# Two nested branches in an expert's further slots: the false arm named as the one to fall through to

## The chip, the cores and the metric

The kernel runs on one core of a Trainium2 chip. The metric is the device time of one execution in microseconds. Before the change three runs took 1592.51, 1592.9 and 1587.8 us, a median of 1592.51.

## The reference

The program is a decoder trunk of two layers over 256 tokens of width 1024, in float32. Each layer has a token mixer (two kinds of attention with a gated merge) and then a feed-forward part; layer 0 has a dense SwiGLU, layer 1 eight SwiGLU experts of inner width 3584, of which each token uses two:

```python
logits = jnp.einsum('bsd,de->bse', h, w_router, preferred_element_type=jnp.float32)
top_v, top_i = lax.top_k(logits, TOP_K)                     # TOP_K = 2 of 8
top_w = jax.nn.softmax(top_v, axis=-1)
combine = jnp.sum(jax.nn.one_hot(top_i, N_EXPERTS) * top_w[..., None], axis=-2)
for e in range(N_EXPERTS):
    y = y + combine[..., e:e + 1] * ((silu(h @ w_gate[e]) * (h @ w_up[e])) @ w_down[e])
```

Each matrix product of an expert is needed only for the tokens that chose it. That number is known only when the program runs. The layer's output goes through a last RMSNorm.

## The kernel before, in words

The change lies in the expert stage, the function `moe`. The router first gives each token a rank among those that chose the same expert, and the number of them per expert (`cnt`). Tokens are gathered into slots by a matmul with a one-hot matrix, up to 128 slots per expert.

Slots are worked in three groups. The first 64 (`S0`) are always computed. Slots 64 to 95 and slots 96 to 127 (groups of `SG` = 32) are computed only where the count asks for them. `more(cs, e, fn)` (L1041) makes the two nested branches for that: the outer one at L1043 is taken where the count is over 64, and inside it `fn(0)` does the first further group; the inner one at L1046 is taken where the count is over 96, and `fn(1)` does the second. The counts are read into registers by `count` (L1035), one set for TensorE (`cPE`) and one for ScalarE and VectorE (`cAD`). There is no else arm in the source. The program still has one: where an arm is skipped, the engine executes an instruction that waits for its earlier work and sets the semaphores that the skipped work would have set (EVENT_SEMAPHORE in the trace).

An expert's inner width is cut in four blocks (`BLOCKS`), the first of 512 columns, the others of 1024. Two experts take turns block by block (0 and 1, then 2 and 3, and so on). One step of this order, at L1275, does for its block:

- `units` (L1067): gate and up projections of the first 64 slots, matmuls at L1060. A block of 1024 does them in two halves.
- `turns_more` (L1264): for the block of two steps ago, transposes of the further slots' activations, under a branch of its own at L1267, and a copy under one at L1129. These two are written with `tc.If` directly and not through `more`.
- `units_more` (L1071): the same projections for the further slots, matmuls at L1087, under `more`, after each half.
- `gated_units`, `gated_more` (L1103): silu and product on ScalarE and VectorE, for further slots under `more`.
- `down` (L1134): the down projection of the block of two steps ago, matmuls at L1147, and for further slots at L1156 under `more`. For the last block of an odd expert the gather of the next experts (L1025) is put between its matmuls.
- `trans` (L1113), and at an expert's end `rows_of` (L1243, its further slots under `more`) and `scatter` (L1234), which adds the rows to the output.

TensorE's part of the loop is in the order written (`in_order`). So TensorE meets the outer branch 11 times for each expert: seven times in `units_more` and four in `down`.

The weights, 1 MB at a time, come through a ring of 17 raw buffers by DMAs that SP issues at L159. A buffer's next DMA is issued (`refill`, after `units_more` and `down`) when the matmuls that read it are through, those under the branches too. An arm that was skipped releases it by its semaphore instruction.

After the loop `overflow` deals with experts of more than 128 tokens, which this input doesn't have, and the final norm writes the output.

Of the kernel before, what the change touches and what calls it, by code (L numbers as in the profile page):

```python
# [51 lines left out]
S0, SG = 64, 32  # L52
# [20 lines left out]
def trunk(  # L73
# [32 lines left out]
    @contextmanager  # L106
    def in_order(*engines):

        had = {i.name for i in nc.cur_bb.bb.instructions}
        yield  # L110
        last = {}
        for i in nc.cur_bb.bb.instructions:
            if i.name in had or i.engine not in engines:
                continue
            if i.engine in last:
                tc.add_manual_dep(i, last[i.engine].name, NOSYNC, reason="in_order")
            last[i.engine] = i
# [327 lines left out]
    for l in range(DEPTH):  # L445
# [32 lines left out]
        if l == 0:  # L478
# [3 lines left out]
            for i in range(14):  # L482
                chunk_ws(dense_w_gate[0], i * 256)
                chunk_ws(dense_w_up[0], i * 256)
                if extra and i >= FA:
                    e = extra.pop(0)
# [500 lines left out]
    def moe(l, pss):  # L987

        with tc.tile_pool(name="mo", bufs=1, reuse_waits="tile") as mo, \
# [50 lines left out]

            def more(cs, e, fn):  # L1041

                with tc.If(cs[e] > S0):  # L1043
                    with in_order(ENG.PE):
                        fn(0)
                        with tc.If(cs[e] > S0 + SG):  # L1046
                            with in_order(ENG.PE):
                                fn(1)

# [21 lines left out]
            def units_more(st):  # L1071

                e, w = st["e"], st["w"]
                xg, o = XG[e - e % 2], (e % 2) * P + S0
                if len(st["p"]) == 2:
                    st["p"] += [pA() for _ in range(2)]
                todo, st["raw"] = st["raw"], []

                def fn(g):
                    H_ = st["p"][2 + g]  # L1080
                    for k, kk, two in todo:
                        for m, raw in enumerate(two):
                            for c in range(2):
                                w0 = (2 * kk + c) * w

                                q = 64 * (m ^ g) + 32 * c
                                mm(H_[q:q + 32, 0:w], xg[:, k, o + SG * g:o + SG * g + SG], raw[:, w0:w0 + w],  # L1087
                                   start=k == 0, stop=k == KT - 1)
                more(cPE, e, fn)
                W.refill(2 * len(todo) // st["nk"])  # L1090
# [12 lines left out]
            def gated_more(st):  # L1103
                e, w, p = st["e"], st["w"], st["p"]
                sg = sm.tile([P, 512], F32, tag="acc", name="sg")

                def fn(g):
                    a, b = slice(64 * g, 64 * g + 64), slice(64 - 64 * g, 128 - 64 * g)
                    act(sg[b, 0:w], p[2 + g][a, 0:w], AF.Silu)  # L1109
                    tt(am[e % 2][a, 0:w], sg[b, 0:w], p[2 + g][b, 0:w], op=OP.mult)  # L1110
                more(cAD, e, fn)
# [22 lines left out]
            def down(st, first, last, ahead=()):  # L1134

                e, n, at = st["e"], st["w"] // P, st["at"]
                if first:
                    Y[e] = [pB() for _ in range(2)]
                y, ym = Y[e]
                todo = []  # L1140
                for h in range(n):
                    raw = W.raw()
                    for i in range(2):
                        c, f = divmod(2 * h + i, n)
                        a, z = first and h == i == 0, last and h == n - 1 and i == 1
                        for d in range(2):
                            mm(y[64 * d:64 * d + 64, :], at[:, f, 64 * c:64 * c + 64],  # L1147
                               raw[:, i * D + 512 * d:i * D + 512 * d + 512], start=a, stop=z)
                        todo.append((raw, i, c, f, a, z))
                    if h < len(ahead):  # L1150
                        ahead[h]()

                def fn(g):
                    for raw, i, c, f, a, z in todo:
                        for d in range(4):
                            mm(ym[32 * d:32 * d + 32, S * g:S * g + S],  # L1156
                               atm[:, f, 64 * g + 32 * c:64 * g + 32 * c + 32],
                               raw[:, i * D + S * d:i * D + S * d + S], start=a and g == 0, stop=z,
                               skip_group_check=True)
                more(cPE, e, fn)  # L1160
                W.refill(n)
# [406 lines left out]
```

## Time and profile before

| what | value |
|---|---|
| runs, median (lowest to highest) | 1592.51 us (1587.8 to 1592.9) |
| profiled execution, its own time | 1589.51 us |
| its span, first to last instruction | 1587.6 us |
| mean granted TensorE clock | 0.986 |
| TensorE busy with matmuls | 1485.0 us, 94% |
| VectorE, ScalarE busy | 582.9 us, 441.5 us |
| moved by DMA | 506.89 MB, 319 GB/s over the span |
| q8, instruction | 132 packets, 2.16 MB |

The span runs from the first to the last instruction of one profiled execution; the execution's own time has what lies around it too. Engines are PE (TensorE matmuls), PEld (its weight loads), DVE (VectorE), ACT (ScalarE), POOL and SP (which issues the weight DMAs). A q behind the engine's name means its sequencer: branches, semaphore instructions and DMA issues, which are not counted as busy. TensorE's sequencer instructions stand under PEldq. COMPARE_BRANCH is the name of each branch instruction, whether it compares or not. L12 is line 12 of the kernel. The queue q8 brings the program's own instructions, in packets of 16 KB.

### The profile page before, as it was taken

The page shows a single profiled execution, that of the slowest core. Times are in us where ns is not written, and L with a number is a line of the kernel's source. Part 1 is how long each engine was busy: PE and PEld are TensorE (multiplying, and loading weights), DVE is VectorE, ACT ScalarE, POOL GpSimd, SP SyncE. Part 2 cuts the span into 40 slices and gives each one's busy share as a digit, 9 for nine tenths or more (in the row PEclk, how much of TensorE's full clock was granted, in tenths as well). Part 3 has the DMA queues.
Part 4 walks back from the last instruction along what each step waited for, and adds up shares of the span by engine and source line. Part 5 has one row for each costly group of instructions (what it writes and reads, how often), then busy time and mean ns, then how long its engine had stood idle before and what let it go on. Part 6 is the DMA issues. An engine that isn't in the chain of part 4 may idle for free. (4 is left out here: it accounts for less than half of the span.)

```text
span 1587.6 us, 24709 instructions
## 1 busy us (share of the span) xinstructions
PE 1485.0 (94%) x10358; PEld 943.6 (59%) x10358; DVE 582.9 (37%) x1024; ACT 441.5 (28%) x693; POOL 84.0 (5%) x96
## 2 busy tenths in 40 slices
PE   6999999999999999989999989999999999899776
PEld 4988989999999899963333533333443333433222
DVE  7698568877757657530000121000030000120003
ACT  3677544333345886230001100000110001000001
POOL 0106020000000240100000000000000000000000
PEclk9999999999999999999999999999999999999998
DMA  9797548888863637789999988999999999999994
GB/s 311 236 304 247 190 136 291 294 286 299 300 220 104 216 113 249 278 318 384 408 409 402 395 323 341 373 369 357 401 379 409 407 408 399 405 408 408 408 407 180
DMA packets 207618, 506.89 MB, mean 319 GB/s; under 512 B 11070, under 2 KB 76892, under 8 KB 207196
## 3 DMA queue, kind: packets, MB, share of 16 engines
q1 hardware_dynamic: 205420, 500.93, 85.0%
q8 instruction: 132, 2.16, 0.6%
q0 software_dynamic: 384, 2.11, 0.4%
q10 hardware_dynamic: 1648, 1.41, 0.3%
q14 instruction: 34, 0.28, 0.0%
HBM read 503.36 MB, written 1.06 MB: 318 GB/s over the span
## 5 line engine op out<-in xcount | busy, mean ns | idle before, releaser
L1060 PE MATMUL pA<-raw,xg 128*64 128x512 f32 (+1 forms) x2048 | 405.2, 547 | 26.8 <-DMA raw<-in_moe_w_up_dram 12.3
L1060 PEld LDWEIGHTS pA<-raw,xg 128*64 128x64 f32 x2048 | 150.0, 138 | 261.7 <-issue 207.9
L667 PE MATMUL pA<-hh,hi 128*128 128x256 f32 x896 | 256.6, 288 | 2.2 <-ACT hh L657 2.2
L668 PE MATMUL pA<-hL,hi 128*128 128x256 f32 x896 | 255.6, 286 | 0.0
L669 PE MATMUL pA<-hh,lo 128*128 128x256 f32 x896 | 255.2, 285 | 0.0
L222 DVE TENSOR_TENSOR lo<-raw,hi 128x2048 fp32r<-128x2048 f32 (+4 forms) x110 | 214.3, 1957 | 85.3 <-ACT hi L216 85.1
L216 ACT ACTIVATE hi<-raw 128x2048 fp32r<-128x2048 f32 (+4 forms) x110 | 180.0, 1645 | 195.5 <-PE pA L668 97.9
L1147 PE MATMUL pB<-raw,at 128*64 128x512 f32 x896 | 208.4, 605 | 18.4 <-DMA raw<-in_moe_w_down_dram 7.3
L667 PEld LDWEIGHTS pA<-hh,hi 128*128 128x128 f32 x896 | 173.4, 194 | 3.0 <-ACT hh L657 2.6
L668 PEld LDWEIGHTS pA<-hL,hi 128*128 128x128 f32 x896 | 174.1, 194 | 0.4 <-DVE hL L660 0.4
L669 PEld LDWEIGHTS pA<-hh,lo 128*128 128x128 f32 x896 | 174.0, 194 | 0.1
L1147 PEld LDWEIGHTS pB<-raw,at 128*64 128x64 f32 x896 | 67.4, 138 | 149.0 <-issue 114.2
L1100 DVE TENSOR_TENSOR sl<-sl,pA 128x512 f32<-128x512 f32 (+1 forms) x32 | 19.9, 621 | 340.8 <-PEq L1043 263.4
L383 DVE SCALAR_TENSOR_TENSOR acc<-raw,sc,acc 128x512 f32<-128x512 f32 x152 | 119.0, 783 | 4.1 <-DMA raw<-in_ada_w_dram 1.5
L1110 DVE TENSOR_TENSOR am<-sg,pA 64x512 f32<-64x512 f32 (+1 forms) x16 | 9.9, 621 | 282.9 <-ACT sg L1109 282.8
L1099 ACT ACTIVATE sl<-pA 128x512 f32<-128x512 f32 (+1 forms) x32 | 17.4, 545 | 345.2 <-PE pA L1060 345.2
L1087 PE MATMUL pA<-raw,xg 128*32 128x512 f32 (+1 forms) x1024 | 100.6, 541 | 0.8 <-ACTq L1129 0.7
L1087 PEld LDWEIGHTS pA<-raw,xg 128*32 128x32 f32 x1024 | 31.1, 110 | 62.5 <-issue 50.2
L1120 ACT COPY at<-pA 128x512 f32<-128x512 f32 (+1 forms) x32 | 17.1, 533 | 174.7 <-PE pA L1118 173.9
L667 PE MATMUL pB<-ah,hi 128*128 128x256 f32 x224 | 63.8, 285 | 0.0
L668 PE MATMUL pB<-al,hi 128*128 128x256 f32 x224 | 63.4, 283 | 0.0
L669 PE MATMUL pB<-ah,lo 128*128 128x256 f32 x224 | 63.3, 283 | 0.0
(315 smaller groups left out, 1639.6 us busy)
## 6 DMA issues: line engine op xcount, KB each, us to landing
raw<-in_moe_w_gate_dram SPq DMA_DIRECT2D x112, 1024.0 KB, 16.3
raw<-in_moe_w_up_dram SPq DMA_DIRECT2D x112, 1024.0 KB, 13.4
raw<-in_moe_w_down_dram SPq DMA_DIRECT2D x112, 1024.0 KB, 15.4
raw<-in_ada_w_dram SPq DMA_DIRECT2D x48, 1024.0 KB, 5.7
raw<-in_w_in_dram SPq DMA_DIRECT2D x30, 1024.0 KB, 5.6
raw<-in_dense_w_gate_dram SPq DMA_DIRECT2D x14, 1024.0 KB, 5.2
raw<-in_dense_w_up_dram SPq DMA_DIRECT2D x14, 1024.0 KB, 5.9
raw<-in_dense_w_down_dram SPq DMA_DIRECT2D x14, 1024.0 KB, 5.5
```

The costliest lines, as they stand in the source:

```text
L216: act(dst(hi), src(raw), AF.Copy)
L222: tt(dst(lo), src(raw), dst(hi), op=OP.subtract)
L383: stt(a, w3[:, k, :], s_, a, op0=OP.mult, op1=OP.add)
L667: mm(o, wh, xh, start=start, stop=False, **kw)
L668: mm(o, wh, xl, start=False, stop=False, **kw)
L669: mm(o, wl, xh, start=False, stop=stop, **kw)
L1060: mm(bank[64 * c:64 * c + 64, 0:w], xg[:, k, o:o + S0], raw[:, w0:w0 + w], start=k == 0, stop=k == KT - 1)
L1087: mm(H_[q:q + 32, 0:w], xg[:, k, o + SG * g:o + SG * g + SG], raw[:, w0:w0 + w], start=k == 0, stop=k == KT - 1)
L1099: act(sl[:, 0:w], p[0][:, 0:w], AF.Silu)
L1100: tt(sl[:, 0:w], sl[:, 0:w], p[1][:, 0:w], op=OP.mult)
L1120: nc.scalar.copy(at[:, 0:n, :], p[:, 0:n * P].rearrange("p (a s) -> p a s", s=P))
L1147: mm(y[64 * d:64 * d + 64, :], at[:, f, 64 * c:64 * c + 64], raw[:, i * D + 512 * d:i * D + 512 * d + 512], start=a, stop=z)
```

## The change

Both branches in `more` get the argument `preferred_fallthrough_block=False`. Its description says: True prefers the true branch next, False the false branch next, None (as before) leaves the selection to the compiler. The condition, the arms and their order in the source stay as they were. `turns_more` and `copy_more` are not changed.

```diff
             def more(cs, e, fn):
 
-                with tc.If(cs[e] > S0):
+                with tc.If(cs[e] > S0, preferred_fallthrough_block=False):
                     with in_order(ENG.PE):
                         fn(0)
-                        with tc.If(cs[e] > S0 + SG):
+                        with tc.If(cs[e] > S0 + SG, preferred_fallthrough_block=False):
                             with in_order(ENG.PE):
                                 fn(1)
```

## Rows read from the trace of the kernel before

**Rows 1.** Windows: stretch, its us, busy us per engine, clock, DMA share, GB/s.

```profile
690.00:930.00 240.00, 226.84 (x1540) 94.59 (x1543) 16.99 (x35) 24.96 (x47) 0.00 (x0) 0.99 0.99 386
930.00:1169.00 239.00, 232.53 (x1744) 93.31 (x1734) 25.96 (x47) 20.67 (x39) 0.00 (x0) 0.99 0.93 358
1169.00:1460.00 291.00, 274.10 (x1578) 106.16 (x1579) 32.12 (x53) 24.83 (x46) 0.00 (x0) 0.99 1.03 405
1460.00:1568.00 108.00, 82.63 (x340) 23.84 (x338) 7.74 (x11) 6.45 (x10) 0.00 (x0) 0.97 0.98 388
```

**Rows 2.** Waits of PE, 690 to 1169: total us, times, longest.

```profile
PE pA L1060 <- PEq L1043: 5.9, 7, 2.1
PE pB L1147 <- issue: 3.0, 1, 3.0
...
PE pA L1060 <- DMA raw<-in_moe_w_gate_dram: 0.5, 1, 0.5
```

**Rows 3.** Waits of SP's queue, 1100 to 1169.

```profile
SPq L159 <- PEq L1046: 12.1, 1, 12.1
```

**Rows 4.** Waits of PE from 1169 on.

```profile
PE pA L1060 <- DMA raw<-in_moe_w_up_dram: 12.3, 11, 1.5
```

**Rows 5.** Branches by line (ns min/median/max, first and last): three until 1169, last whole.

```profile
L1043 PEldq COMPARE_BRANCH  x45: 65/70/3775, 701.1 to 1163.7; - x45
L1043 PEldq EVENT_SEMAPHORE  x22: 51/51/51, 702.8 to 1141.6; - x22
L1046 PEldq EVENT_SEMAPHORE  x12: 51/51/51, 714.3 to 1168.4; - x12
L1267 PEldq COMPARE_BRANCH  x24: 65/184/303, 718.3 to 1161.0; - x24
...
L1043 PEldq EVENT_SEMAPHORE  x55: 51/51/51, 702.8 to 1572.6; - x55
```

**Rows 6.** Timeline of PE: start, us, matmuls, [idle before], two stretches.

```profile
746.57 7.09 PE L1060 MATMUL pA<-raw,xg 128*64 128x512 f32 x32 [0.46 <-PEq L1046]
753.59 3.64 PE L1087 MATMUL pA<-raw,xg 128*32 128x512 f32 x32
757.73 3.65 PE L1147 MATMUL pB<-raw,at 128*64 128x512 f32 x16 [0.50 <-PEq L1046]
...
1046.46 7.09 PE L1060 MATMUL pA<-raw,xg 128*64 128x512 f32 x32 [0.58 <-PEq L1043]
...
1053.69 7.09 PE L1147 MATMUL pB<-raw,at 128*64 128x512 f32 x32
```

**Rows 7.** Single branches and one semaphore of PE, by line, in short stretches.

```profile
L1043 PEldq COMPARE_BRANCH  x1: 342/342/342, 1049.1 to 1049.1; - x1
...
L1046 PEldq COMPARE_BRANCH  x1: 174/174/174, 757.5 to 757.5; - x1
...
L1043 PEldq COMPARE_BRANCH  x1: 214/214/214, 1046.1 to 1046.1; - x1
...
L1043 PEldq COMPARE_BRANCH  x1: 2987/2987/2987, 774.7 to 774.7; - x1
...
L1043 PEldq COMPARE_BRANCH  x1: 366/366/366, 915.5 to 915.5; - x1
...
L1043 PEldq COMPARE_BRANCH  x1: 330/330/330, 1129.1 to 1129.1; - x1
...
L1043 PEldq EVENT_SEMAPHORE  x1: 51/51/51, 1132.2 to 1132.2; - x1
```

**Rows 8.** DMA queues, 915.9 to 921.8: packets, MB, share.

```profile
q8 instruction: 1, 0.02, 1.2%
```

**Rows 9.** Timeline of PE around 907, 921 and 1132.

```profile
907.15 7.13 PE L1060 MATMUL pA<-raw,xg 128*64 128x256 f32 x64
...
921.76 7.06 PE L1147 MATMUL pB<-raw,at 128*64 128x512 f32 x23 [3.01 <-issue]
...
1132.82 7.84 PE L1060 MATMUL pA<-raw,xg 128*64 128x256 f32 x64
```

**Rows 10.** Windows, 921.9 to 925.2, columns as in rows 1.

```profile
921.90:925.20 3.30, 3.30 (x9) 1.24 (x10) 0.00 (x0) 0.00 (x0) 0.00 (x0) 0.50 1.03 410
```

## The prediction

> **What bounds the kernel now.** I read the busy table by stretch first, since the branches that change all lie in the expert stage, from 690 us on. In [rows 1] the reader is to see three regimes. Until 1169 TensorE is 95 to 97% busy (226.84 of 240, 232.53 of 239) and the DMA rate is 386, then 358 GB/s. From 1169 to 1460 the rate is 405 with TensorE at 94%. From 1460 on TensorE falls to 82.63 of 108, while the share of DMA stays at 0.98. Second, TensorE's waits until 1169: the costliest are 5.9 us behind its own sequencer (PEq) and 3.0 us of "issue", and a weight transfer costs 0.5 [rows 2]. So weights are there early, the ring of raw buffers is full, and the next transfer waits until TensorE frees a buffer. Third, the waits of SP, which issues the weights: the longest before 1169 is 12.1 us for TensorE's sequencer at L1046 [rows 3], whose last semaphore of that stretch stands at 1168.4 [rows 5]. After that the weights run at 405 GB/s until 1460, and behind it TensorE waits for them (12.3 us for w_up alone, [rows 4]). **So a delay of TensorE before 1168.4 passes one for one to the end; a delay behind it has slack.**
>
> **What the change does.** I take it that the order of the arms in the instruction stream turns round. Today the taken arm follows the branch. L1267, which stays as it is, shows it: its 16 calls until 1169 make 24 branches [rows 5], 16 compares and 8 jumps, one at the end of each taken arm, so the taken arm stands first and jumps over the other. An arm not taken is thus: the compare jumps (200 to 450 ns mostly), and then a semaphore instruction waits until TensorE is empty. With the false arm first it is: the compare falls through (65 to 70 ns, the minimum in [rows 5]), the semaphore waits, and then a jump leads over the true arm. The number of jumps is the same, but the jump moves from ahead of the wait to behind it.
>
> That matters because the sequencer runs ahead. In [rows 7] a compare stands at 1049.1 and takes 342 ns, while the matmuls queued before it run to 1046.46 + 7.09 = 1053.55 [rows 6]: the jump is hidden under 4.5 us of queued work, and the next matmul follows at 1053.69, 0.14 us later. The inner branch shows what a jump behind the semaphore costs: there the arm not taken ends with a jump over two instructions (174 ns at 757.5, [rows 7]), and TensorE idles 0.50 us, in others 0.46 [rows 6]. The difference, 0.32 us, is my price.
>
> **The sum up to 1168.4.** The rows count 22 outer arms not taken and 12 inner ones, by their semaphores [rows 5].
> - Six of the 22 follow an arm not taken at L1267, with the engine empty already; with the first branch of the stage they are the 7 waits of 5.9 us in [rows 2]. There the compare's jump is exposed today (214 ns in [rows 7], idle 0.58 in [rows 6]). It is exchanged for a compare that falls through and a jump: 65 ns and its spacing more, about 0.13 us. 6 x 0.13 = 0.8 us.
> - The other 16: 0.32 us each, and where the target lies in the next packet of code 0.12 more, from the two sizes of a jumping compare (214 and 342 ns, [rows 7]). The jumps lead over 128 or 256 instructions (32 or 64 matmuls for each of the two groups of slots, each with its weight load), so I give the 0.12 to half. 16 x 0.38 = 6.1 us. From both sides: 1.6 less than nothing, if the sequencer prepares the jump while it waits and the compare's 0.1 us goes; 0.45 each, 7.2 us, if all targets are far. The nearest row is the inner arm, so 6.1.
> - The 12 inner ones have their jump behind the semaphore already. It now leads over one group of slots instead of two instructions: 0.12 in a third of them, 0.5 us.
> - Arms taken (45 less 22, 23 outer calls): their compare now jumps, but with a full queue in front of it, and the jump at their end goes. Nothing. The cover is the matmuls before each, such as 3.64 us in [rows 6]; without it, 23 x 0.2 = 4.6 us.
> - ScalarE and VectorE take the same branches but are busy 25 and 17 of 240 us [rows 1]. Nothing; if TensorE ever waited for one of these jumps it would be 0.2 us.
>
> The jumps come to 0.8 + 6.1 + 0.5 = 7.4 us.
>
> **Code that is not there yet.** Some compares take far longer: 2987 ns at 774.7 [rows 7], up to 3775 until 1169 [rows 5]. What stands behind it is seen best where TensorE itself stops. After the jump at 915.5 (366 ns, [rows 7]) the matmuls of the down projection stop in their middle; one packet of the instruction queue arrives [rows 8], and they go on at 921.76 after 3.01 us idle [rows 9], 5.86 us behind the jump's end at 915.9. I read from it that entering a packet of code starts the fetch of the packet after it, usable some 5.8 us later. Most such waits are hidden today under the 4.5 us of queued matmuls, and so I do not add the long compares up. When the jump comes behind the drain, the next jump is a group of matmuls later (7.09 us in [rows 6]), over 5.8, and the packet is there. The exception is code that crosses a packet's end soon after a jump. The compare at 1129.1 (330 ns, [rows 7]) entered a packet at 1129.4; 5.8 us later is 1135.2, and the 64 matmuls from 1132.82 take 7.84 us where the same 64 take 7.13 [rows 9]: I read that they reach the packet's end about then. The semaphore of that arm stands at 1132.2 [rows 7]. With the jump behind it, the packet is entered at 1132.6 and the next is there at 1138.4: some 2.8 us without work.
>
> [...] The place is worth 4.5 us if the packet ends where I think. I count half, 2.3 us, because I know the end from that one row. At 915.5 the jump moves behind its semaphore by 0.4 us more than is counted: 0.4.
>
> **Sum:** 7.4 + 2.3 + 0.4 = 10.1 us. Behind 1169 lie another 33 outer arms not taken (55 semaphores in all, [rows 5]), 33 x 0.38 = 12.5 us, beside waits for weights that shrink instead (12.3 us for w_up alone, [rows 4]). Between 1169 and 1460 a part could starve the ring again, 0 to 4 us; I take nothing. The profiled execution took 1589.5 us (span 1587.6), so its own sum is 1599.6 us. The median of the runs, 1592.5, lies 3.0 above that execution, their mean, 1591.1, lies 1.6 above; I place the forecast at 1601 us.
>
> [...]
>
> **Rivals.**
> 1. *No change.* The order of the arms stays (a preference, not an order), or the jump is prepared during the wait, or the full ring gives the microseconds back. For it: the taken arms stand first without being asked, so the lowering has a rule of its own. Against it: naming a preference can do nothing else than set this order. Not slower: minus 1.6 to plus 4.7 us, 1588 to 1595 us. Chance 0.2.
> 2. *Faster, by the fetch.* [...] Chance 0.08.
> 3. *The hidden waits come out.* If a packet is fetched only when the jump asks for it, every long compare is exposed. With a third of the 22 at 2.4 us (an estimate between the 0.3 and the 3.8 of [rows 5, 7]) that is 17 us on top of 7.4: 1614 us and more. The same, and larger, if the true arms are put far away: each of 23 taken calls would wait 5.8 less 4.5 us going and coming, 60 us. Against it: at 915.5 the 5.8 us count from the jump before, not from the stop. Chance 0.08.
>
> **Numbers.** The forecast's own case, 1596 to 1608 us, has 0.64. Differences under 0.3%, 4.8 us, are what a measurement of this kernel can't tell from none. Slower by more than that: 0.64 and 0.08, 0.72. Faster 0.08, within 0.3% 0.20. The range 1591 to 1610 leaves out the second and third rival and the lower part of the first.
>
> **What would show it.** In the profile after, compares at L1043 on TensorE that are not taken should show 65 to 70 ns, each followed by its semaphore and a second branch of 170 to 350 ns; the idle before the next matmul should be 0.45 to 0.6 us. TensorE should pass the point that is at 1168.4 now about 10 us later, and from there on run as before. An idle of 2 to 3 us should lie some 5.8 us behind the jump of the down projection with the gathers. The step is wrong if compares keep their 200 ns and more, and the one-for-one claim is wrong if TensorE is 10 us late at that point and the end is not.

## The result, and the profile after

| | before | after |
|---|---|---|
| median (lowest to highest, 5 runs each) | 1592.9 us (1587.8 to 1594.48) | 1606.32 us (1601.2 to 1607.16) |
| profiled execution, its own time | 1589.51 us | 1606.76 us |
| its span | 1587.6 us | 1605.0 us |
| instructions | 24709 | 24785 |

The ratio after to before is 1.0091, with a 95% interval of 1.0075 to 1.0107: some 14 us slower. 1601 had been forecast, with a range of 1591 to 1610 and 0.72 on slower.

The first view of the kernel after is the branches of TensorE's sequencer by line, to be read against [rows 5]: nanoseconds min/median/max, then the first and last start. The first two lines are L1043 until 1185 us, the third and fourth L1046, the last is L1043 over the whole span.

```profile
L1043 PEldq COMPARE_BRANCH  x67: 64/211/2011, 704.6 to 1179.8; - x67
L1043 PEldq EVENT_SEMAPHORE  x22: 51/51/51, 706.3 to 1157.2; - x22
...
L1046 PEldq COMPARE_BRANCH  x35: 64/201/309, 716.6 to 1184.6; - x35
L1046 PEldq EVENT_SEMAPHORE  x12: 51/51/51, 718.2 to 1184.5; - x12
...
L1043 PEldq EVENT_SEMAPHORE  x55: 51/51/51, 706.3 to 1589.6; - x55
```

45 branches have become 67: one more for each of the 22 arms not taken. The semaphores date the two executions. The first at L1043 goes from 702.8 to 706.3. The first changed branch of TensorE starts 1.7 us ahead of it in both kernels, and over all the kernels below, changed or not, this semaphore lies between 702.1 and 707.6, so I do not count these 3.5 us as the change's. The twelfth at L1046 goes from 1168.4 to 1184.5, 12.6 us more than that. The last at L1043 goes from 1572.6 to 1589.6, 13.5 more. **The loss is made before 1168.4 and then stands to the end.** That twelfth semaphore at L1046 is called the point below.

One arm not taken in after, single branches in short stretches: the compare falls through, the semaphore waits, the jump comes behind it.

```profile
L1043 PEldq COMPARE_BRANCH  x1: 69/69/69, 730.0 to 730.0; - x1
...
L1043 PEldq EVENT_SEMAPHORE  x1: 51/51/51, 734.5 to 734.5; - x1
...
L1043 PEldq COMPARE_BRANCH  x2: 64/178/293, 734.7 to 735.2; - x2
...
L1043 PEldq COMPARE_BRANCH  x1: 2011/2011/2011, 739.0 to 739.0; - x1
...
L1043 PEldq COMPARE_BRANCH  x1: 297/297/297, 1145.6 to 1145.6; - x1
```

The jump at 734.7 takes 293 ns, and TensorE idles 0.69 us where it idled 0.30. The one at 739.0 takes 2011 ns, and TensorE idles 2.26 us where the idle was 0.15 (from 730.72 + 3.65 to 734.52). The same place before:

```profile
730.72 3.65 PE L1147 MATMUL pB<-raw,at 128*64 128x512 f32 x16 [0.30 <-PEq L1043]
734.52 0.63 PE L1118 MATMUL pA<-ident,sl 128*128 128x128 f32 x4
```

Before had seven compares of 1.4 to 3.8 us at L1043 until the point: TensorE is not idle during six of them, and for 0.31 us of the 2.89 of the seventh (1138.7); after has this one long jump. The waits of PE in after from 690 to 1185 (total us, times, longest) answer to [rows 2]:

```profile
PE pA L1060 <- PEq L1043: 6.3, 6, 2.2
PE pB L1147 <- PEq L1043: 5.0, 8, 0.7
PE pB L1147 <- issue: 3.3, 1, 3.3
PE pA L1118 <- issue: 2.3, 1, 2.3
PE pA L1060 <- issue: 2.2, 1, 2.2
PE pB L1147 <- PEq L1046: 2.1, 4, 0.6
```

The down projection (L1147) now waits 5.0 us for PEq L1043, 0.8 before, and there are three single stops of "issue" where there was one. A stop is an idle time of 2 us or more for which the profile shows nothing that was waited for. The timeline shows them (start, us, matmuls, [idle before]), the first and last stop and the old one between them:

```profile
735.11 3.65 PE L1147 MATMUL pB<-raw,at 128*64 128x512 f32 x16 [0.69 <-PEq L1043]
741.02 1.11 PE L1118 MATMUL pA<-ident,sl 128*128 128x128 f32 x4 [2.26 <-issue]
...
928.34 2.36 PE L1147 MATMUL pB<-raw,at 128*64 128x512 f32 x9 [0.68 <-PEq L1043]
934.01 5.37 PE L1147 MATMUL pB<-raw,at 128*64 128x512 f32 x23 [3.31 <-issue]
...
1146.58 2.37 PE L1060 MATMUL pA<-raw,xg 128*64 128x256 f32 x18
1151.20 5.34 PE L1060 MATMUL pA<-raw,xg 128*64 128x256 f32 x46 [2.24 <-issue]
```

The jump at 734.7 ended at 734.94. One packet of the instruction queue follows between 738.4 and 739.6, and the next jump, which stood waiting from 738.96, ends at 740.97, 6.0 us behind the end of the first. The packet begins to arrive at 738.47, 0.49 us ahead of the start of this jump, so it is not this jump that asked for it. At the other two stops the jump's end lies 5.7 us (928.28 to 934.01) and 5.3 us (1145.94 to 1151.20) ahead of the matmuls that go on. The DMA queues of after from 738.4 to 739.6 (packets, MB, share of 16 engines):

```profile
q8 instruction: 1, 0.02, 5.6%
```

Behind the point the waits for weights answer to [rows 4] (waits of PE from 1185 on):

```profile
PE pA L1118 <- issue: 6.3, 1, 6.3
PE pB L1147 <- DMA raw<-in_moe_w_down_dram: 5.4, 8, 1.4
PE pB L1147 <- PEq L1043: 5.0, 9, 0.7
PE pA L1060 <- DMA raw<-in_moe_w_up_dram: 4.6, 4, 1.9
```

The 12.3 us for w_up are down to 4.6. I summed the idle times of TensorE behind each kind of arm not taken, from the first semaphore at L1043 to the point (in us; "other" has no such semaphore in it; the clock column is half of the time at a granted clock of 0.50, and the last column is the length of the whole stretch). Half is counted, since TensorE does 8 matmuls of L1147 in 3.0 us of before at 0.50 (from 922.0) and 15 at 1.00 (from 925.6).

| | outer, 22 | inner, 12 | L1267 alone | other | clock | length |
|---|---|---|---|---|---|---|
| before | 8.8 | 5.8 | 1.0 | 3.5 | 3.4 | 465.6 |
| after | 18.0 | 6.6 | 1.1 | 5.9 | 3.4 | 478.2 |

The differences, 9.2 + 0.8 + 0.1 + 2.4, give 12.5 of the 12.6 us, which leaves 0.1 for all else, the arms taken among it. Of the 9.2, 2.0 are the long jump at 739.0.

### The profile page after: what moved, and what is told of

The parts are those of the page before. It is cut to its first block, busy times and chain, and to the rows that moved or that the text cites. A ratio compares the mean times of both kernels' runs of the same rounds, so it can differ in the third digit from the quotient of the medians.

```text
span 1605.0 us, 24785 instructions
## 1 busy us (share of the span) xinstructions
PE 1487.3 (93%) x10358; PEld 940.8 (59%) x10358; DVE 584.1 (36%) x1024; ACT 440.9 (27%) x693; POOL 82.9 (5%) x96
## 5 line engine op out<-in xcount | busy, mean ns | idle before, releaser
L1147 PE MATMUL pB<-raw,at 128*64 128x512 f32 x896 | 205.8, 602 | 23.1 <-PEq L1043 10.0
L1147 PEld LDWEIGHTS pB<-raw,at 128*64 128x64 f32 x896 | 62.3, 137 | 156.2 <-issue 132.0
L1100 DVE TENSOR_TENSOR sl<-sl,pA 128x512 f32<-128x512 f32 (+1 forms) x32 | 19.9, 621 | 337.2 <-PEq L1043 286.4
## 6 DMA issues: line engine op xcount, KB each, us to landing
raw<-in_moe_w_up_dram SPq DMA_DIRECT2D x112, 1024.0 KB, 11.1
```

The source lines that it names most:

```text
L1100: tt(sl[:, 0:w], sl[:, 0:w], p[1][:, 0:w], op=OP.mult)
L1147: mm(y[64 * d:64 * d + 64, :], at[:, f, 64 * c:64 * c + 64], raw[:, i * D + 512 * d:i * D + 512 * d + 512], start=a, stop=z)
```

## The experiments

Each was timed in turn with the kernel before. "Late at the point" is the length of the stretch above less 465.6 us, "late at the end" the same to the last semaphore at L1043. Both come from the one execution that was profiled, the medians from all.

| | median, us | before, us | ratio (95% interval) | late at the point | late at the end |
|---|---|---|---|---|---|
| after | 1606.32 | 1592.9 | 1.0091 (1.0075 to 1.0107) | 12.6 | 13.5 |
| e1_outer | 1600.77 | 1590.55 | 1.0059 (1.0037 to 1.0082) | 6.0 | 6.0 |
| e2_inner | 1592.72 | 1590.55 | 1.0008 (0.9996 to 1.002) | 0.7 | 1.3 |
| e3_pe | 1605.65 | 1590.55 | 1.0092 (1.0073 to 1.0112) | 12.7 | 13.7 |
| e4_ad | 1590.24 | 1590.55 | 1.0001 (0.9988 to 1.0014) | -1.8 | -2.5 |
| e5_first | 1606.59 | 1590.77 | 1.01 (1.008 to 1.0121) | 11.1 | 11.8 |
| e6_last | 1592.15 | 1590.77 | 1.0012 (0.9999 to 1.0026) | -1.5 | -0.1 |
| e7_turn | 1606.2 | 1590.77 | 1.0099 (1.0078 to 1.012) | 12.9 | 15.8 |
| e8_early | 1582.87 | 1590.77 | 0.9953 (0.9935 to 0.9971) | -10.3 | -10.1 |
| e9_shift_before | 1585.8 | 1590.99 | 0.9975 (0.9963 to 0.9987) | -7.3 | -7.4 |
| e10_shift_after | 1613.95 | 1590.99 | 1.0156 (1.0126 to 1.0185) | 11.8 | 19.7 |
| e11_early_false | 1606.95 | 1590.99 | 1.0102 (1.0077 to 1.0127) | 9.7 | 16.3 |
| e12_early36 | 1585.75 | 1591.0 | 0.9969 (0.9956 to 0.9981) | -6.1 | -6.1 |

### Which of the two branches

e1_outer has the argument on the outer branch alone, e2_inner on the inner alone.

```diff
# e1_outer, against the kernel after
-                        with tc.If(cs[e] > S0 + SG, preferred_fallthrough_block=False):
+                        with tc.If(cs[e] > S0 + SG, preferred_fallthrough_block=None):
# e2_inner, against the kernel after
-                with tc.If(cs[e] > S0, preferred_fallthrough_block=False):
+                with tc.If(cs[e] > S0, preferred_fallthrough_block=None):
```

> Only the outer branch names the false arm. Theory (a jump behind the drained wait costs 0.3 to 0.45 us on TensorE, and entering code later lets it run dry at some packets' ends): the outer arms not taken pay as in the changed kernel, some +6.9 us until 1168; the inner arms not taken lose the jump that they have before, since the outer false arm no longer stands behind them, 12 x 0.31 = -3.7 us, and their idle goes from 0.46 to 0.15; the stops for code add 3 to 5. Together +6 to +8 us. Rival, that the time comes from the inner branch: under +3 us.

> Only the inner branch names the false arm. Theory: its jump stood behind the wait before and only leads further now, 12 x 0.04 to 0.1: +0.5 to +1.5 us, not told from none. Rival, that any branch so marked costs alike (34 arms not taken until 1168, 12 of them inner): +4 us or more.

Most of the loss is the outer branch's. In e1 the outer arms idle 18.1 us, as in after. The inner arms idle only 3.1 us in place of 5.8, a median of 0.18 us each: their jump over two instructions is gone (34 branches at L1046 until the point, 46 before, and none behind a semaphore). The time is up by 10.2 us between medians, more than the 6 to 8 forecast; the trace, 6.0 late, has no spell of low clock in the stretch (a spell is a stretch at a granted clock of 0.50), which gives 3.4 us back against before. The waits of PE for L1046 in e1, 690 to 1180 (total us, times), show the inner arms:

```profile
  PE pB L1147: 0.7, 4
  PE pA L1118: 0.7, 3
  PE pA L1060: 0.4, 2
  PE pA L1229: 0.2, 1
```

e2 alone adds 0.75 us of idle, the jump that now leads over a group of slots; its interval holds no change. Taken with the outer branch, the inner one costs the 3.5 us between 3.1 and 6.6. With the 3.4 us of clock, that is what lies between e1 and after at the point (6.0 and 12.6).

### Which engines

e3_pe and e4_ad split the change by the registers that are compared: TensorE alone, or ScalarE and VectorE alone.

```diff
# e3_pe; e4_ad has cAD in place of cPE
-                with tc.If(cs[e] > S0):
+                with tc.If(cs[e] > S0, preferred_fallthrough_block=False if cs is cPE else None):
...
-                        with tc.If(cs[e] > S0 + SG):
+                        with tc.If(cs[e] > S0 + SG, preferred_fallthrough_block=False if cs is cPE else None):
```

> Both branches marked, but only where TensorE branches; ScalarE and VectorE keep the order of before. Theory: all of the change's loss, +12 to +14 us. Rival, that the chain over ScalarE and VectorE (silu, product, copy) is late: clearly less, +0 to +8 us.

> Both branches marked, but only where ScalarE and VectorE branch; TensorE keeps the order of before. Theory: no change, within 2 us. Rival, that these engines' branches carry the loss: +5 us or more.

All of it is TensorE's: e3 is 13.7 us late in its trace and 15.1 between medians (12 to 14 forecast), e4 not at all. e3 repeats even the three stops at their places. The -1.8 of e4 is one spell of low clock: before has two spells of 3.4 us in this stretch, e4 has one.

### Which part of the stage

e5_first has the argument for experts 0 to 3, e6_last for experts 4 to 7, whose branches lie mostly behind the point.

```diff
# e5_first; e6_last has e >= 4
-                with tc.If(cs[e] > S0):
+                with tc.If(cs[e] > S0, preferred_fallthrough_block=False if e < 4 else None):
...
-                        with tc.If(cs[e] > S0 + SG):
+                        with tc.If(cs[e] > S0 + SG, preferred_fallthrough_block=False if e < 4 else None):
```

> Both branches marked for experts 0 to 3 alone, whose work ends about the point that was at 1168. Theory (a delay until there passes one for one, a delay behind it has slack): nearly all of the loss, +11 to +14 us. Rival, that every arm not taken counts alike wherever it lies: 22 of 55, +5 to +6 us.

> Both branches marked for experts 4 to 7 alone. Theory: TensorE falls behind by 10 us or so until 1460 and gets it back from its waits for weights: 0 to +2 us. Rival, that every arm counts alike: 33 of 55, +7 to +9 us.

The first half of the experts costs as much as the whole change (11.8 us late in the trace, 15.8 between medians, 11 to 14 forecast), the second half nothing that can be told from none. TensorE in e6 does get late behind the point, by up to 10.9 us, and the waits for weights take it up. The waits of PE in e6 from 1169 on, against 12.3 and 7.3 us for w_up and w_down in before:

```profile
PE pA L1118 <- issue: 6.5, 1, 6.5
PE pA L1060 <- PEq L1043: 6.5, 8, 0.9
PE pB L1147 <- DMA raw<-in_moe_w_down_dram: 5.5, 6, 1.8
PE pB L1147 <- PEq L1043: 5.1, 9, 0.7
PE pA L1060 <- DMA raw<-in_moe_w_up_dram: 4.2, 4, 1.4
```

### More of the same: the branch at L1267 too

```diff
# e7_turn, against the kernel after
-                with tc.If(cPE[st["e"]] > S0):
+                with tc.If(cPE[st["e"]] > S0, preferred_fallthrough_block=False):
```

> The changed kernel with the branch at L1267 marked too: one suspected cost more in 20 places, 8 of them until 1168. There the jump is hidden today and would come behind a drained wait. Theory: 8 x 0.3 = +2.5 us beyond the changed kernel, +15 to +17 us against the kernel before. Rival, that the loss is only the stops for code: as the changed kernel, +13 us.

Its time can't be told from that of after, so it settles nothing by itself. In its trace the eight arms not taken at L1267 before the point idle 1.8 us more, 0.23 each, but 1.7 us less are lost to the clock.

### The other way: fewer waits behind an empty engine

e8_early leaves the branches as before. It does the count reads and the transposes of the further slots (with the branch at L1267) ahead of the block's projections, so that a wait on an empty engine is followed by queued matmuls and not by the next branch.

```diff
# e8_early, against the kernel before; three places of the step at L1275
+                    if i == 1 and e % 2 == 1 and e + 1 < NE:
+                        count(e + 1)
+                        count(e + 2)
+                    if prev is not None:
+                        turns_more(prev)
...
-                    if prev is not None:
-                        turns_more(prev)
...
-                    if i == 1 and e % 2 == 1 and e + 1 < NE:
-                        count(e + 1)
-                        count(e + 2)
```

> The kernel before, with the order of the arms as it was, but the branch at L1267 and the loads of the next two counts moved ahead of a step's first matmuls. Theory: where an arm not taken follows another with the engine empty (six times until 1168) the jump gets cover back, -0.3 to -0.5 us each, and the 2.1 us idle with its 1.7 us of lower clock at 980 go: -3 to -7 us. Rival, that exposed jumps cost nothing at the end: no change.

It beats both kernels, by a little more than the 3 to 7 us forecast. The outer arms idle 4.4 us in place of 8.8, and those at L1267 1.8 in place of 1.0, 3.6 us less together. The stop of 3.0 us at 918.8, which the forecast did not count on, is gone, with both spells of low clock (3.4 us). Some 1.1 us of other idle come in, and 1.4 us less are taken by the same matmuls.

### The same two kernels with the code shifted

e9_shift_before and e10_shift_after are the kernels before and after with 16 more calls of the warm-up at their start, in the program 32 matmuls and their weight loads, 64 instructions (24773 and 24849 in place of 24709 and 24785), so that all that follows lies elsewhere in the packets of code. Nothing else differs.

```diff
-WD = 20
+WD = 36
```

> The kernel before with 16 more warm-up matmuls at the program's start (WD 36 for 20), in a wait for the first weights: every later instruction of TensorE moves by 64 in its packet of 16 KB. Theory: the time changes by 2 us or less, but the stop of 3 us in the down projection at 918, if it is a wait for code, is not at that place or not of that length. Rival (it waits for something of the program): it stays, 2.9 to 3.3 us.

> The changed kernel with the same shift by 64 instructions. Theory: the idle of 0.45 to 0.65 us at every arm not taken stays (18 us over the 22 outer ones until 1168, less the stop among them), while the three stops of 2 to 3 us move, go or come elsewhere; +7.5 to +15 us against the kernel before. Rival, that the stops belong to the work at those places: the same three stops, +13 us.

The shift alone makes the kernel before 0.25% faster, 5.2 us between medians, where 2 or less had been forecast. Its stop at 918 is gone (it was [rows 9]), and so is the low clock behind it [rows 10]. The timeline of e9:

```profile
917.77 0.40 PE L1240 MATMUL pA<-yl,oht 128*128 128x512 f32 x1
918.32 7.09 PE L1147 MATMUL pB<-raw,at 128*64 128x512 f32 x32
```

And its windows, 921 to 925 us (columns as in [rows 1]):

```profile
921.00:925.00 4.00, 4.00 (x22) 1.47 (x18) 0.00 (x0) 0.00 (x0) 0.00 (x0) 1.00 1.02 407
```

The kernel after gets slower by the same shift, 28 us above e9 and 23 above before: the forecast of 7.5 to 15 missed it, by the stops. Of the three stops of after until the point, those of 2.26 and 2.24 us are gone. That of the down projection at 930 has become a jump that waits at its start, a second such jump stands at 997.7, and there is a stop of 4.9 us in the middle of four transposes. The two jumps, and then the timeline of e10:

```profile
L1043 PEldq COMPARE_BRANCH  x1: 2922/2922/2922, 922.9 to 922.9; - x1
...
L1043 PEldq COMPARE_BRANCH  x1: 2181/2181/2181, 997.7 to 997.7; - x1
```

```profile
1067.06 0.44 PE L1229 MATMUL pA<-idr,oh 128*128 128x128 f32 x2 [0.57 <-PEq L1043]
1067.34 0.52 PE L1118 MATMUL pA<-ident,sl 128*128 128x128 f32 x3
1072.79 0.47 PE L1118 MATMUL pA<-ident,sl 128*128 128x128 f32 x1 [4.94 <-issue]
```

The jump ahead of it ended at 1067.00, again 5.8 us before the matmuls go on. **The stops are the position's; the jumps are not:** the outer arms of e10 idle 20.2 us until the point, or 15.1 without its two long jumps, where after has 16.0 without its one. Against e9, with 8.5, these jumps cost 6.7 us; against before, after's cost 7.2. Behind the point e10 loses 7.9 us more to the end: it idles 9.2 us in two stops alone there.

```profile
PE pB L1147 <- issue: 9.2, 2, 5.1
```

### The argument on the faster order, and that order elsewhere

e11_early_false is e8 with the argument on both branches, as in the change. e12_early36 is e8 with `WD = 36`.

```diff
# e11_early_false, against e8_early
-                with tc.If(cs[e] > S0):
+                with tc.If(cs[e] > S0, preferred_fallthrough_block=False):
...
-                        with tc.If(cs[e] > S0 + SG):
+                        with tc.If(cs[e] > S0 + SG, preferred_fallthrough_block=False):
```

> The earlier L1267 and counts together with the change. Theory: against the version with them earlier alone (1582.9) all 22 outer arms not taken now pay the whole price, 22 x 0.3 to 0.45, 6.6 to 9.9, and 1 us for the inner ones, stops for code 0 to 5: 1591 to 1598 us, +1 to +7 us against the kernel before. Rival, that the gain of moving them comes from hiding what the change exposes: the loss nearly gone, 1583 to 1587 us.

> The moved counts and turns_more of e8 (no preference named), with WD = 36 in place of 20, so that all code behind the warm-up matmuls lies 64 instructions later. Theory: the jumps that e8 hides under queued matmuls stay hidden wherever the code lies, so about 4 us of its gain over the kernel before (the idle behind L1043 and L1267) stand; the stops of 2 to 3 us depend on the position, and a new one or two may come in or none. Forecast 1583 us, range 1579 to 1590: not slower than e9's 1585.8 by more than a stop. Rival: e8's gain was its position alone; then this one has the stops that e8 lost, the 3 us at the gather's down projection and 2 us at the counts with their clock, and comes out at 1588 to 1595.

e11 misses its forecast of 1591 to 1598: it is 24 us above e8. Until the point it is 19.9 us later than e8. Of these the 22 outer arms take 11.6 (4.4 to 16.0), 3.6 of it in two long jumps and 8.0 in the others, 0.37 each; a stop at 929 takes 2.0; and the clock takes 5.1, where e8 lost none there. The branches of e11 at L1043 until 1179, and what waited for them:

```profile
L1043 PEldq COMPARE_BRANCH  x67: 64/207/2172, 701.2 to 1171.5; - x67
...
  PE pB L1147: 5.9, 8
  PE pA L1118: 3.5, 3
  PE pA L1060: 3.2, 6
  PE pA L1229: 1.3, 2
```

The forecast had the jumps right and allowed 0 to 5 us for stops, of which 5.6 came until the point. It left out the 5.1 us of clock, and 6.5 us more that e11 loses behind the point against e8.

e12 has less of a gain in its trace than e8 (6.1 us at the end in place of 10.1), though the intervals of their ratios overlap. So do those of e12 (0.9969) and e9 (0.9975): at this position the order gains nothing that can be measured. The outer arms still idle 3.6 us less than in e9 (4.8 against 8.5), those at L1267 1.0 more (1.8 against 0.8), but a stop of 2.4 us comes in at 1125.9 (waits of PE in e12 until 1170):

```profile
PE pA L1125 <- issue: 2.4, 1, 2.4
```

So at the arms the order saves 2.6 us here and 3.6 in e8. The rest of e8's gain is stops and clock, and that it belongs to where the code lies is argued from the shifts, not shown. e8 is the fastest version run, though part of its lead hangs on what stands ahead of it.

## Why the prediction was right, step by step

- **The order of the arms turns round: right.** The compare of an arm not taken takes 64 to 72 ns, one of the 22 takes 93, and a jump follows its semaphore (69, 51 and 293 ns in the fences above).
- **The jumps, 7.4 us: right.** Measured are 7.2 for the outer arms (9.2 less the long jump) and 0.8 for the inner, together 8.0. Both parts of the outer sum hold: the six arms behind L1267 idle 0.8 us more (0.8 forecast), the other 16 some 6.4 without the long jump (6.1). Until the point the jumps of the outer arms in after take 176 to 426 ns, the long one of 2011 left out, where 170 to 350 had been named, and such an arm idles some 0.33 us more (7.2 us over 22). The 0.12 us for targets in the next packet of code was the author's estimate from two sizes: no run shows where a target lies. Arms taken and the other two engines were put at nothing, and e4_ad shows nothing for these engines.
- **The stops, 2.7 us: mis-sized.** Of the predicted places both came. Behind the down projection with the gathers TensorE stops for 2.24 us (2.8 forecast, and 1.7 for the clock, the two counted half as 2.3). At the old stop it is 3.31 in place of 3.01 (0.4 forecast). What failed is the sentence that "the next jump is a group of matmuls later (7.09 us in [rows 6]), over 5.8, and the packet is there". The first block of an expert has half the columns and so a group of 3.65 us, which stands in the same rows. The jump behind one of them waits 2.0 us. The stops come to 2.0 + 2.24 + 0.3 = 4.5 us, and the sum to 12.5 in place of 10.1.
- **The size was in part luck.** The stops hang on where the code lies. Had it lain where e10 has it, the change would have cost 28 us (e10 against e9) and the time would have been above the range (e10's median is 1613.95). What the prediction knew was the jumps, 7 to 8 us at both positions.
- **The clock.** No run shows the 1.7 us of clock in the 4.5 us of the place behind the gathers: there the granted clock is 1.00 from 1151.2 on. The spell after the new stop at 739 is there, but the old one at 921.8 is not, although the stop before it has grown. Windows of after, behind the second, third and first of the stops:

```profile
934.00:937.40 3.40, 3.39 (x16) 1.54 (x17) 0.00 (x0) 0.00 (x0) 0.00 (x0) 1.00 1.02 408
1151.20:1154.60 3.40, 3.40 (x32) 3.13 (x33) 0.00 (x0) 0.00 (x0) 0.00 (x0) 1.00 1.03 411
741.00:744.30 3.30, 3.27 (x10) 1.49 (x12) 0.00 (x0) 0.58 (x1) 0.00 (x0) 0.50 1.05 413
```

  The second spell is the same in both, behind an idle of 2.1 us that ends at 982.0 before and one of 2.2 that ends at 992.7 after. Two spells in before, two in after: nothing on balance.
- **One for one until 1168.4, slack behind it: right, up to a limit that was not named.** e5_first and e6_last show both halves. In after 10.8 us less are idle in waits without a branch behind the point, against 13.3 more at outer arms. In e10, where 16.7 us are added behind the point until the place that is at 1465 in before, 7.9 come out at the end. The slack is that of the waits for weights, and no more.
- **The rivals.** No change and faster fall with e1_outer and e3_pe, both slower with intervals above 1.003. The third, every hidden wait coming out, falls as a whole (1614 us and more): until the point one long jump stands where seven long compares were. But the stops are the part that was under-counted, and a jump that waits some 6 us itself is seen once behind the point (5957 ns, below).

What stays open: neither the place of a packet's end nor what starts its transfer was read from a run. That the stops are waits for code is the author's inference, from the one packet that lands ahead of the end of each of the stops at 741.0, 934.0 and 1151.2 in after and 1072.8 in e10 (1.3 to 1.5 us ahead), and from their moving when the code is shifted. Nor does the prediction's reading, that a packet's fetch starts when the one before it is entered, fit every row. One jump of after waits its whole 5957 ns itself, though TensorE had gone on 3.0 us earlier, at 1382.4, 1.4 us behind the landing of a packet. No packet of the instruction queue q8 arrives from 1381.1 to 1388.8, and then one does until 1390.0. The jump, and the matmuls around it:

```profile
L1043 PEldq COMPARE_BRANCH  x1: 5957/5957/5957, 1385.4 to 1385.4; - x1
...
1382.41 2.79 PE L1147 MATMUL pB<-raw,at 128*64 128x512 f32 x11 [0.61 <-issue]
1391.52 0.66 PE L1118 MATMUL pA<-ident,sl 128*128 128x128 f32 x2 [6.32 <-issue]
```

There the 6 us count from the start of the jump. It lies behind the point, where the waits for weights take it up. Why it differs is not shown.

## What to carry to other kernels

Here a branch that jumps was hidden while TensorE had matmuls queued (0.15 us of idle at 12 of the 16 outer arms that do not follow L1267) and exposed behind a wait that empties the engine (0.44 to 0.79 us at the same arms, the long jump left out); so keep the jump ahead of the wait, which here is what the lowering does without being asked. Behind a jump look 5 to 6 us further on in the timeline: here TensorE stopped there for 2.26 us (until 741.0), behind a group of 3.65 us that ended in another jump, and for 2.24 us (until 1151.2) in the middle of a straight run of matmuls. Before an order of code is called better by half a per cent, shift the code by some instructions and time both again.

## What the runs showed of the hardware

- From the end of a jump to the end of the stop behind it, four stops took 5.3 to 6.0 us (5.3 at 1151.2, 5.7 at 934.0 and 6.0 at 741.0 in after, 5.8 at 1072.8 in e10), with one 16 KB packet of the instruction queue in between, which lands 1.3 to 1.5 us before the engine goes on (739.54 and 740.97, 932.70 and 934.01, 1149.75 and 1151.20 in after, 1071.46 and 1072.79 in e10). The DMA engines move 406 to 409 GB/s meanwhile in after.
- 64 instructions that do nothing to the expert stage, put in at the kernel's start, change the whole time by -0.25% in one kernel and, measured against the same kernel before, by +0.65% (1.0091 to 1.0156) in the other.
- In after, idles of 2.26 us (until 741.0) and 2.23 us (until 992.7) were followed by 3.4 us at a granted clock of 0.50 (from 740.95 and 993.54), and idles of 3.31 us (until 934.0) and 2.24 us (until 1151.2) by none.
